# The last RMS norm of a decoder trunk: column-wise Newton steps, and one of four final products on GpSimd

## The chip, the cores and the metric

The kernel runs on one core of a Trainium2 chip. The metric is the device time of one execution, in microseconds (us); of several runs the median is given. The profile is of one execution, taken by the hardware profiler. Its engines are called PE (TensorE), DVE (VectorE), ACT (ScalarE), POOL (GpSimd) and SP (SyncE), and L143 means line 143 of the kernel.

## The reference

The reference computes one layer of a decoder trunk for 1024 tokens of width 1024 in float32: an attention part of three head groups, a gated MLP with a short convolution, a gated per-layer embedding, and a last RMS norm. Only the end matters here:

```python
gate = jax.nn.sigmoid(_rmsnorm(r, ple_norm[i]).astype(dt) @ w_ple_gate[i])
r = r + (p[i] @ w_ple_proj[i]) * gate
...
return _rmsnorm(r, final_norm).astype(dt)
```

where `_rmsnorm` multiplies each token's row by one over the root of its mean square (plus 1e-6), and by a gain per feature.

## The kernel before, in words

The activations are held feature-major: eight tiles of 128 features by 1024 tokens (`r[d]`, two of them in each tile `r2[i]`). Every float32 matrix product is made of three matmuls on split operands (`mm3`, L115 to L119).

The last stage works on three pieces of the tokens, 512, 256 and 256 wide (`PIECES`). `embed` (L1134) computes a piece: for each of the eight feature tiles d it makes the gate's matmuls on PE into a PSUM tile `pg` (L1163), and `gate_in` (L1140) scales the result, takes the sigmoid on ACT, multiplies by the embedding, adds it to `r[d]` (L1145), gathers the squares (L1147, the last tile's at L1149), and multiplies `r[d]` by the gain of the last norm on ACT (L1151).

`finish` (L1174) then ends a piece. It is called for a piece while the next piece's matmuls run (by `before()` behind the second feature tile, L1169), and for the last piece alone at the very end (L1188). It does the following:

- `rms_sum` (L146): matmuls with a column of ones bring the sum of squares of each token into a PSUM tile, 128 tokens on the partitions and one column per 128 tokens (L152, L154). So a piece of 256 tokens has two columns. L157 makes the mean.
- `rsqrt` (L132): one over the root on VectorE by a first guess from the bits (L135, L137), a halved and negated input `h` (L139), and three Newton iterations of three operations each (L141 to L143), each of which needs the one before it. The working tile is `t`, the result is `y`.
- `rms_spread` (L161): a matmul for each column against the identity puts the result, one factor per token, on all 128 partitions of a PSUM tile (L166).
- Four products on VectorE, each over two feature tiles (128 partitions x 2 x 256 elements), multiply `r2` by that PSUM tile in place (L1179), and after each SP issues the store of 256 KB (L1181).

`rsqrt` is also used with four and eight columns, earlier in the kernel and in the first piece. The framework lets every engine work through its own queue in order; it chooses the order of the queues by priorities, which follow the order in which the program states the operations, and puts a wait where two operations touch the same tile and one of them must come first.

Other lines that the prediction speaks of: L536 and L537 (part of the rotary embedding; ACT copies a PSUM tile into `t`, VectorE multiplies the same PSUM tile into `z`), L619 and L620 (ACT copies, and VectorE masks, a PSUM tile into the two halves of `pT`), L346 (the running states of the two recurrent heads, one with a decay per partition read from SBUF as the tile `fs`, the other with a constant), L605 (a two-column operation with a scalar per partition), L781 (a sum of squares, on GpSimd in earlier stages).

Of the kernel before, what the change touches and what calls it, by code (L numbers as in the profile page):

```python
# [22 lines left out]
ALU = mybir.AluOpType  # L23
# [3 lines left out]
P = 128  # L27
T = 1024
D = 1024
KD = D // P  # L30
# [5 lines left out]
PIECES = ((0, 512), (512, 768), (768, 1024))  # L36
# [39 lines left out]
def trunk(ctx: ExitStack, tc: tile.TileContext, a, out, dbg):  # L76
    nc = tc.nc
    V, S, G, TE = nc.vector, nc.scalar, nc.gpsimd, nc.tensor
# [4 lines left out]
    ps = ctx.enter_context(tc.tile_pool(name="ps", bufs=1, space=PSUM))  # L83
# [11 lines left out]
    def half(h):  # L95
        return slice(h * H2, (h + 1) * H2)
# [35 lines left out]
    def rsqrt(y, v, n, pool):  # L132
        h = pool.tile([P, n], F32, tag="rq_h", bufs=2, name="rq_h")
        t = pool.tile([P, n], F32, tag="rq_t", bufs=2, name="rq_t")
        V.tensor_scalar(out=t.bitcast(I32), in0=v.bitcast(I32), scalar1=1, scalar2=None,  # L135
                        op0=ALU.logical_shift_right)
        V.tensor_scalar(out=y.bitcast(I32), in0=t.bitcast(I32), scalar1=-1.0, scalar2=float(0x5F3759DF),  # L137
                        op0=ALU.mult, op1=ALU.add)
        V.tensor_scalar(out=h, in0=v, scalar1=-0.5, scalar2=None, op0=ALU.mult)  # L139
        for _ in range(3):  # L140
            V.tensor_tensor(out=t, in0=y, in1=y, op=ALU.mult)  # L141
            V.tensor_tensor(out=t, in0=t, in1=h, op=ALU.mult)
            V.scalar_tensor_tensor(out=y, in0=t, scalar=1.5, in1=y, op0=ALU.add, op1=ALU.mult)  # L143


    def rms_sum(acc, cols, name, rest=None):  # L146

        n = (cols.stop - cols.start) // P
        pt = b1(f"ss_{name}")
        for c in range(n):  # L150
            ac = slice(cols.start + c * P, cols.start + (c + 1) * P)
            TE.matmul(pt[:, c:c + 1], acc[:, ac], ones[:, 0:1], start=True, stop=rest is None)  # L152
            if rest is not None:
                TE.matmul(pt[:, c:c + 1], rest[:, ac], ones[:, 0:1], start=False, stop=True)  # L154
        v = cp.tile([P, 8], F32, tag="rb_v", bufs=2, name=f"rb_v{name}")
        y = cp.tile([P, 8], F32, tag="rb_y", bufs=2, name=f"rb_y{name}")
        V.tensor_scalar(out=v[:, :n], in0=pt[:, :n], scalar1=1.0 / D, scalar2=EPS, op0=ALU.mult, op1=ALU.add)  # L157
        rsqrt(y[:, :n], v[:, :n], n, cp)
        return y[:, :n]
# [9 lines left out]
    def rms_bc(acc, rs, cols, name, rest=None):  # L169

        y = rms_sum(acc, cols, name, rest)
        n = y.shape[-1]
        for c0 in range(0, n, 4):
            m = min(4, n - c0)
            pb = rms_spread(y[:, c0:c0 + m], name)
            if rs is None:
                return pb
            S.copy(rs[:, cols.start + c0 * P:cols.start + (c0 + m) * P], pb)
# [25 lines left out]
    with tc.high_priority(offset=100000):  # L204
# [4 lines left out]
        for k in range(KD):  # L209
            x = xs[k]  # L210
# [9 lines left out]
            for h in range(2):  # L220
                S.mul(hi[:, half(h)], x[:, half(h)], col(C_G1 + k))
                V.scalar_tensor_tensor(out=lo[:, half(h)], in0=x[:, half(h)], scalar=col(C_G1 + k),
                                       in1=hi[:, half(h)].bitcast(F32), op0=ALU.mult, op1=ALU.subtract)
# [8 lines left out]
            for n in range(NS):  # L232
                for h in range(2):
                    w = slice(n * P, n * P + P)
# [79 lines left out]
    def head_out(po, dst):  # L314

        pv = po.rearrange("p (c d) -> p c d", c=NC)
        sq = ap.tile([P, NC, 64], F32, tag="kt", bufs=1, name="hsq")
        S.square(sq, pv)
        v = ap.tile([P, NC], F32, tag="hv", bufs=2, name="hv")
        y = ap.tile([P, NC], F32, tag="hy", bufs=2, name="hy")  # L320
        V.tensor_reduce(out=v, in_=sq, axis=AX.X, op=ALU.add)
        V.tensor_scalar(out=v, in0=v, scalar1=1.0 / 64, scalar2=EPS, op0=ALU.mult, op1=ALU.add)
        rsqrt(y, v, NC, ap)
        V.tensor_tensor(out=dst.rearrange("p c (e d) -> p (c e) d", e=2), in0=pv,
                        in1=y[:, :, None].to_broadcast([P, NC, 64]), op=ALU.mult)
# [434 lines left out]
    def f4(tag, name, shape=(P, T), dt=F32):  # L760
        if tag == "big":
            return big.tile(list(shape), dt, tag="big", name=name)
        if tag in ("wraw", "whi", "wlo"):
            return wp.tile(list(shape), dt, tag=tag, bufs=1 if tag == "wraw" else 2, name=name)
        return fp.tile(list(shape), dt, tag=tag, bufs=BUFS[tag], name=name)
# [73 lines left out]
    for d in range(KD):  # L839
        out_tile_half(d, 1)  # L840
        if d == 0:
            y = rms_sum(acc2, half(0), "r0")
# [8 lines left out]
    for n, (h, i, d) in enumerate((h, i, d) for h in range(2) for i in range(2) for d in range(4)):  # L851
# [9 lines left out]
        if n == 1:  # L861
            with tc.high_priority(offset=100):
                y = rms_sum(acc2, half(1), "r1")
# [170 lines left out]
    def weights_down(src, n, name):  # L1034
        with tc.high_priority(offset=400):
            raw, hi, lo = [f4(t, f"wd{name}{t}", (P, n, P), dt)
                           for t, dt in (("wraw", F32), ("whi", F32R), ("wlo", F32R))]
            nc.sync.dma_start(raw, src)
            hl(hi, lo, raw)
        return hi, lo  # L1040
# [4 lines left out]
    def streamed(f, again):  # L1045
        return h3_parts(f, again, *[f4("r", f"{c}3{f}{again}", dt=F32R) for c in "hl"])

    def kept(f):
        if f == NF - 1 or f == NF - 2:
            t = f4("hx", f"h3{f}", (P, 2, T), F32R)  # L1050
            return h3_parts(f, 0, t[:, 0], t[:, 1])
        return h3_parts(f, 0, *[f4("big", f"{c}3{f}", dt=F32R) for c in "hl"])
# [5 lines left out]
    r2 = []  # L1058
# [39 lines left out]
    for f in range(NF):  # L1098
        x = streamed(f, 0) if f < NR else kept(f)
        h3[f] = x  # L1100
        w = weights_down(a["w_dn0"][f], 4, f"a{f}")
# [9 lines left out]
    for n, f in enumerate([*range(NR, NR + NE), *range(NR)]):  # L1111
        x = streamed(f, 1) if f < NR else h3[f]
        w = weights_down(a["w_dn1"][f], 4, f"b{f}")
# [7 lines left out]
    for d in range(4):  # L1121
        w = weights_down(a["w_dn2"][d], NK, f"c{d}")
# [51 lines left out]
    def finish(n, t0, t1):  # L1174
        c = slice(t0, t1)
        w = t1 - t0
        pb = rms_bc(acc4[0][:, c], None, slice(0, w), f"f{n}", last_sq[n])
        for d in range(0, KD, 2):
            V.tensor_tensor(out=r2[d // 2][:, :, c], in0=r2[d // 2][:, :, c],  # L1179
                            in1=pb[:, None, :].to_broadcast([P, 2, w]), op=ALU.mult)  # L1180
            nc.sync.dma_start(out[d:d + 2, :, c].rearrange("d p t -> p d t"), r2[d // 2][:, :, c])  # L1181

    last_sq = []
    before = None
    for n, (t0, t1) in enumerate(PIECES):
        embed(n, t0, t1, before)
        before = functools.partial(finish, n, t0, t1)
# [116 lines left out]
```

## Time and profile before

| what | value |
| --- | --- |
| median of three runs | 1291.88 us (lowest 1289.81, highest 1574.35) |
| profiled execution, its own time | 1289.75 us |
| span from first to last instruction | 1288.0 us |
| mean granted clock of PE | 0.995 |
| instructions | 16291 |

A row of the timeline gives the start and the length in us, the engine, the line, the operation, output and inputs with their shapes, and in brackets the time that the engine stood idle before it and what ended this. A row of one line's view gives the shortest, median and longest duration in ns, and under it what the engine waited for (us in total, times, or us, times, longest). A row of the stretches gives for each stretch its length, each engine's busy time, the clock granted to PE, the busy share of the 16 DMA engines and the GB/s they moved. A row of the DMA issues gives the number of transfers, the size of one and the time from issue to landing.

### The profile page before, as it was taken

The numbers are of one execution on the slowest core, as the hardware profiler recorded it, in microseconds if no ns is written. First come the engines' busy times: TensorE is split into PE (matmuls) and PEld (weight loads), VectorE is DVE, ScalarE is ACT, GpSimd is POOL, SyncE is SP. The second block draws the span as 40 slices with busy tenths as digits, with TensorE's granted clock in tenths as the row PEclk, the third lists the DMA queues.
The fourth block names the chain that finished last, engine by engine and source line by source line (L and its number), as shares of the span: only waits on it lengthen the run. The fifth ranks groups of instructions, "written<-read, shape, count | busy, mean of one in ns | idle before, by whom it ended". The sixth has DMA issues, their size and how long they took to land.

```text
span 1288.0 us, 16291 instructions
## 1 busy us (share of the span) xinstructions
PE 1262.1 (98%) x6330; PEld 1058.9 (82%) x6330; DVE 838.7 (65%) x1410; ACT 536.9 (42%) x842; POOL 103.8 (8%) x113
## 2 busy tenths in 40 slices
PE   9999999999999999999999999999999999999996
PEld 7888888888888887788788888888888888888896
DVE  7986967567676477967776776677456123346576
ACT  7324143257674256544444344334245123334432
POOL 2000000012111231000000000000000021001010
PEclk9999999999999999999999999999999999999998
DMA  7110110111013745222223122123457216323132
GB/s 249 50 34 17 34 33 19 49 33 34 17 34 122 284 135 180 82 98 77 87 82 98 66 82 98 68 88 100 162 163 255 72 53 201 106 90 115 41 107 83
DMA packets 42239, 122.31 MB, mean 95 GB/s; under 512 B 5169, under 2 KB 7729, under 8 KB 42161
## 3 DMA queue, kind: packets, MB, share of 16 engines
q1 hardware_dynamic: 32032, 89.14, 21.3%
q0 software_dynamic: 8544, 30.41, 6.4%
q10 hardware_dynamic: 1584, 1.71, 0.4%
q8 instruction: 50, 0.82, 0.3%
q14 instruction: 29, 0.23, 0.1%
HBM read 97.13 MB, written 24.12 MB: 94 GB/s over the span
## 4 chain that ended last, share of the span: by engine, by line
PE 69%; issue 11%; POOL 2%; DVE 1%; ACT 1%; DMA 0%; DVEq 0%; POOLq 0%; ACTq 0%
PE d L118 6%; PE d L117 6%; PE d L119 6%; PE gb L117 3%; PE gb L118 3%; PE gb L119 3%; PE pg L117 2%; PE gd L117 2%; PE gd L118 2%; PE pg L119 2%; PE gd L119 2%; PE pg L118 2%; PE ga L118 2%; PE ga L119 2%; PE ga L117 2%
## 5 line engine op out<-in xcount | busy, mean ns | idle before, releaser
L117 PE MATMUL ga<-b,whig 128*128 128x512 f32 x176 | 68.9, 392 | 0.3
L119 PE MATMUL ga<-b,wlog 128*128 128x512 f32 x176 | 68.6, 390 | 0.5 <-DVE wlog L773 0.5
L117 PE MATMUL gb<-b,f 128*128 128x512 f32 x176 | 68.7, 390 | 0.0
L118 PE MATMUL ga<-b,whig 128*128 128x512 f32 x176 | 68.6, 390 | 0.0
L119 PE MATMUL gb<-b,f 128*128 128x512 f32 x176 | 68.5, 389 | 0.0
L118 PE MATMUL gb<-b,f 128*128 128x512 f32 x176 | 68.5, 389 | 0.0
L117 PE MATMUL pg<-hp,hpg 128*128 128x256 f32 (+1 forms) x192 | 61.7, 321 | 0.0
L773 DVE TENSOR_TENSOR l<-h3r,h 128x1024 fp32r<-128x1024 f32 x32 | 38.8, 1224 | 34.5 <-ACT h L772 34.5
L119 PE MATMUL pg<-hp,lpg 128*128 128x256 f32 (+1 forms) x192 | 61.0, 318 | 0.0
L118 PE MATMUL pg<-lp,hpg 128*128 128x256 f32 (+1 forms) x192 | 61.0, 318 | 0.0
L772 ACT CAST h<-h3r 128x1024 fp32r<-128x1024 f32 x34 | 35.3, 1050 | 41.1 <-PE d L118 19.7
L955 ACT ACTIVATE cv<-cv 128x1024 f32<-128x1024 f32 x22 | 23.4, 1062 | 67.8 <-DVE cv L953 67.7
L946 DVE TENSOR_TENSOR us<-us,s 128x512 f32<-128x512 f32 x21 | 14.5, 691 | 50.9 <-ACT us L945 50.9
L987 POOL DMA_DIRECT2D h3d<-us x22 | 11.8, 535 | 417.6 <-DVE us L986 417.6
L781 POOL TENSOR_TENSOR acc<-acc,sq 128x512 f32<-128x512 f32 (+1 forms) x15 | 29.0, 1936 | 166.1 <-ACT sq L780 165.8
L117 PEld LDWEIGHTS ga<-b,whig 128*128 128x128 f32 x176 | 33.0, 188 | 8.9 <-ACT s L972 1.5
L945 ACT COPY us<-gd 128x512 f32<-128x512 f32 x22 | 12.9, 588 | 64.2 <-DMA h3d<-us 63.6
L119 PEld LDWEIGHTS ga<-b,wlog 128*128 128x128 f32 x176 | 33.0, 188 | 7.9 <-DVE wlog L773 1.0
L117 PEld LDWEIGHTS gb<-b,f 128*128 128x128 f32 x176 | 33.0, 188 | 7.4 <-DVE us L939 0.3
L119 PEld LDWEIGHTS gb<-b,f 128*128 128x128 f32 x176 | 33.0, 188 | 6.9
L118 PEld LDWEIGHTS pg<-lp,hpg 128*128 128x128 f32 x192 | 36.6, 191 | 2.6 <-DVE lp L1081 0.2
L119 PEld LDWEIGHTS pg<-hp,lpg 128*128 128x128 f32 x192 | 36.6, 190 | 2.5
(778 smaller groups left out, 3859.2 us busy)
## 6 DMA issues: line engine op xcount, KB each, us to landing
wu<-w_gu SPq DMA_DIRECT2D x22, 512.0 KB, 3.5
wg<-w_gu SPq DMA_DIRECT2D x22, 512.0 KB, 3.5
h3d<-us POOLq DMA_DIRECT2D x22, 512.0 KB, 2.9
h3r<-h3d SPq DMA_DIRECT2D x22, 512.0 KB, 3.7
wr_wo<-w_out SPq DMA_DIRECT2D x16, 512.0 KB, 3.7
h3r<-h3d POOLq DMA_DIRECT2D x12, 512.0 KB, 3.8
x<-xT SPq DMA_DIRECT2D x16, 256.0 KB, 5.4
r<-xT SPq DMA_DIRECT2D x16, 256.0 KB, 7.2
```

What stands on the lines that cost most here:

```text
L117: TE.matmul(o, wh, xh, start=first, stop=False, skip_group_check=on)
L118: TE.matmul(o, wh, xl, start=False, stop=False, skip_group_check=on)
L119: TE.matmul(o, wl, xh, start=False, stop=last, skip_group_check=on)
L772: S.copy(hi, src)
L773: e.tensor_tensor(out=lo, in0=src, in1=hi.bitcast(F32), op=ALU.subtract)
L781: e.tensor_tensor(out=acc[:, cols], in0=acc[:, cols], in1=sq[:, cols], op=ALU.add)
L945: S.copy(u1, bank["d"])
L946: V.tensor_tensor(out=u1, in0=u1, in1=s1, op=ALU.add)
L955: S.activation(cv, cv, AF.Gelu_apprx_tanh)
L987: G.dma_start(h3_dram[f], us)
```

## The change

Two edits, both at the end of a piece.

In `rsqrt`, when there are at most two columns (the second and the third piece of the last norm), the two operations y*y and (y*y)*h are replaced by one for each column, which takes that column of `h` as a scalar per partition: (y*h)*y. The third operation of an iteration stays as it is.

In `finish`, for the last piece only, ScalarE first copies the spread factors from PSUM into an SBUF tile `ps`. The product of feature tiles 6 and 7 is made by GpSimd with this copy, and its store is issued by ScalarE's queue. It is stated second, so the order in the program is 0, 6, 2, 4; the other three products stay on VectorE with the PSUM tile, and their stores on SP.

```diff
         for _ in range(3):
-            V.tensor_tensor(out=t, in0=y, in1=y, op=ALU.mult)
-            V.tensor_tensor(out=t, in0=t, in1=h, op=ALU.mult)
+            if n <= 2:
+                for c in [slice(i, i + 1) for i in range(n)]:
+                    V.scalar_tensor_tensor(out=t[:, c], in0=y[:, c], scalar=h[:, c], in1=y[:, c],
+                                           op0=ALU.mult, op1=ALU.mult)
+            else:
+                V.tensor_tensor(out=t, in0=y, in1=y, op=ALU.mult)
+                V.tensor_tensor(out=t, in0=t, in1=h, op=ALU.mult)
             V.scalar_tensor_tensor(out=y, in0=t, scalar=1.5, in1=y, op0=ALU.add, op1=ALU.mult)
...
         pb = rms_bc(acc4[0][:, c], None, slice(0, w), f"f{n}", last_sq[n])
-        for d in range(0, KD, 2):
-            V.tensor_tensor(out=r2[d // 2][:, :, c], in0=r2[d // 2][:, :, c],
-                            in1=pb[:, None, :].to_broadcast([P, 2, w]), op=ALU.mult)
-            nc.sync.dma_start(out[d:d + 2, :, c].rearrange("d p t -> p d t"), r2[d // 2][:, :, c])
+        if n == len(PIECES) - 1:
+            ps = f4("ws", "rs4")[:, :w]
+            S.copy(ps, pb)
+        for d in (0, 6, 2, 4) if n == len(PIECES) - 1 else range(0, KD, 2):
+            e, x = (G, ps) if d == 6 and n == len(PIECES) - 1 else (V, pb)
+            e.tensor_tensor(out=r2[d // 2][:, :, c], in0=r2[d // 2][:, :, c],
+                            in1=x[:, None, :].to_broadcast([P, 2, w]), op=ALU.mult)
+            (S if e is G else nc.sync).dma_start(out[d:d + 2, :, c].rearrange("d p t -> p d t"), r2[d // 2][:, :, c])
```

## The prediction

> **What bounds the kernel now.** I read the page's first part, then the timeline of the last 15 us, then the DMA engines by half microsecond, then single lines.
>
> ```profile
> span 1288.0 us, 16291 instructions
> PE 1262.1 (98%) x6330; PEld 1058.9 (82%) x6330; DVE 838.7 (65%) x1410; ACT 536.9 (42%) x842; POOL 103.8 (8%) x113
> ```
>
> TensorE is the bound, so an edit on another engine can only count where TensorE waits for it. That is the end, after the last gate product:
>
> ```profile
> 1277.37 0.57 PE L154 MATMUL ss_f<-ones,pt 128*128 128x1 f32 x2
> ...
> 1278.17 0.17 DVE L135 TENSOR_SCALAR rq_t<-rb_vf 128x2 int32<-128x2 int32 x1
> 1278.25 0.16 DVE L139 TENSOR_SCALAR rq_h<-rb_vf 128x2 f32<-128x2 f32 x1
> 1278.37 0.17 DVE L137 TENSOR_SCALAR rb_yf<-rq_t 128x2 int32<-128x2 int32 x1
> 1278.58 0.16 DVE L141 TENSOR_TENSOR rq_t<-rb_yf 128x2 f32<-128x2 f32 x1
> 1278.77 0.16 DVE L142 TENSOR_TENSOR rq_t<-rq_t,rq_h 128x2 f32<-128x2 f32 x1
> 1278.97 0.16 DVE L143 SCALAR_TENSOR_TENSOR rb_yf<-rq_t,rb_yf 128x2 f32<-128x2 f32 x1
> 1279.16 0.16 DVE L141 TENSOR_TENSOR rq_t<-rb_yf 128x2 f32<-128x2 f32 x1
> ...
> 1280.14 0.16 DVE L143 SCALAR_TENSOR_TENSOR rb_yf<-rq_t,rb_yf 128x2 f32<-128x2 f32 x1
> ...
> 1280.45 1.19 PE L166 MATMUL rb_f<-ident,rb_yf 128*128 128x128 f32 x4 [2.51 <-DVE rb_yf L143]
> 1281.68 2.48 DVE L1179 TENSOR_TENSOR rr<-rr,rb_f 128x512 f32<-128x512 f32 x4 [1.38 <-PE rb_f L166]
> 1282.43 2.13 SPq L1181 DMA_DIRECT2D out<-rr  x4
> ```
>
> Here everything is one chain. A step that depends on the one before starts 0.195 us after it (0.16 of work, 0.035 of handover); one that doesn't starts 0.08 after it (L135, L139). An iteration is three dependent steps, 1278.58 to 1279.16: 0.585 us, and three make 1.755. Then the spread on TensorE, four products 0.60 apart (2.48 less the last one's 0.69, over three), and a store behind each. What ends the chain is not the last product:
>
> ```profile
> 1283.50:1284.00 0.50, 0.00 (x0) 0.00 (x0) 0.50 (x2) 0.00 (x0) 0.00 (x0) 0.50 1.05 342
> ...
> 1285.50:1286.00 0.50, 0.00 (x0) 0.00 (x0) 0.00 (x0) 0.00 (x0) 0.00 (x0) 0.50 1.01 348
> 1286.00:1286.50 0.50, 0.00 (x0) 0.00 (x0) 0.00 (x0) 0.00 (x0) 0.00 (x0) 0.50 0.81 279
> ```
>
> The last two columns are the busy share of the 16 DMA engines and GB/s. From 1283.5, before the third product is done, to about 1286.4 the engines are full. The stores' queue and the last store:
>
> ```profile
> q1 hardware_dynamic: 1088, 1.05, 44.7%
> ```
>
> ```profile
> 1284.19 0.37 SPq L1181 DMA_DIRECT2D out<-rr  x1
> ```
>
> ```profile
> out<-rr SPq DMA_DIRECT2D x1, 256.0 KB, 2.7
> ```
>
> 1.05 MB at 345 GB/s take 3.0 us. The last store, issued at 1284.19, lands 2.7 later at 1286.9; 1.1 us of closing waits follow. So the end is set by when the first store is issued (1282.43), plus 4.47 us of a stream at full rate, not by the products behind it.
>
> **The change part by part.**
>
> *The copy to SBUF.* GpSimd takes its factor from a copy that ScalarE makes of the spread result, and in the program that copy stands ahead of all four products. Do the products on VectorE, which read the same PSUM tile, wait for it? In L537 VectorE reads a PSUM tile that ScalarE's L536 copies, and writes another tile than L536 does; in L619 and L620 ScalarE and VectorE read one tile too.
>
> ```profile
> L537 DVE TENSOR_TENSOR ck<-z_ck,cosT x4: 691/692/692, 123.3 to 204.1; 128x512 f32<-128x512 f32 x4
> ...
>   ACT tbq L536: 13.9, 7
> ```
>
> ```profile
> 300.34 0.37 ACT L619 COPY pT<-tb 128x256 f32<-128x256 f32 x1 [0.97 <-PE tb L617]
> ...
> 300.74 0.42 DVE L620 TENSOR_TENSOR pT<-tb,tmask 128x256 f32<-128x256 f32 x1 [0.87 <-ACT pT L619]
> ```
>
> L537's own data came from TensorE alone, and yet it waited seven times, 13.9 us, for ScalarE's reading of the tile. So two readers of a PSUM tile go one after the other, in the order of the program. L619 is just the copy that is added (128x256 from PSUM): VectorE starts 0.40 after it. Bounds: 0 if the products may start beside it, +0.60 if the handover costs half as much again as the copy. I take +0.40: first product at 1282.08, first store at 1282.83.
>
> The Trainium skill (PSUM — Partial Sum Buffer, PSUM bank collisions raise a hardware error) says that two engines may not touch one bank and the same partitions at once, reading against reading included. The trace agrees by L537's 13.9 us; with the rule the term is 0.40, without it 0, and it lowers the chance of the rival that lets them run side by side.
>
> *Newton with two columns.* L141 and L142 go, and two column steps come, each with a scalar per partition read from SBUF; the count of instructions stays nine. If these cost what plain ones do, an iteration is 0.08 + 0.195 + 0.195 = 0.47 and three save 0.35. But the scalar read from SBUF costs:
>
> ```profile
> L346 DVE SCALAR_TENSOR_TENSOR sta<-sta,fs,ua x24: 273/280/289, 111.2 to 184.8; 64x64 f32<-64x64 f32 x24
> L346 DVE SCALAR_TENSOR_TENSOR stc<-stc,uc x24: 202/220/226, 207.6 to 250.8; 64x64 f32<-64x64 f32 x24
> ```
>
> ```profile
> 292.72 0.35 DVE L605 TENSOR_SCALAR bmx<-sb,nsink 128x2 f32<-128x2 f32 x2
> ```
>
> ```profile
> 292.72 0.21 DVE L605 TENSOR_SCALAR bmx<-sb,nsink 128x2 f32<-128x2 f32 x1
> ```
>
> The same operation takes 0.06 us more with such a scalar (280 against 220 ns). L605 is a two-column operation with one: 0.21 long, and the second of a pair ends 0.35 after the first began, so it began some 0.13 after it. An iteration is then 0.35 to the end of the second column step, 0.035 of handover and 0.195 of the last step: 0.58, against 0.585. I take -0.02 for all three. Bounds: -0.35 without the extra, and +0.35 if the second column step has to wait for the first, since both write tile t (2 x 0.255 + 0.195 = 0.705 an iteration).
>
> *The same Newton in the piece before*, whose chain runs beside TensorE:
>
> ```profile
> 1259.52 0.15 DVE L143 SCALAR_TENSOR_TENSOR rb_yf<-rq_t,rb_yf 128x2 f32<-128x2 f32 x1
> 1259.57 0.28 PE L119 MATMUL pg<-hp,lpg 128*128 128x256 f32 x1
> ...
> 1259.81 0.68 PE L166 MATMUL rb_f<-ident,rb_yf 128*128 128x128 f32 x4
> ```
>
> Matmuls there start 0.12 apart, and the spread starts 0.24 after the one before, so TensorE stands 0.12 for the chain. An earlier result gains at most 0.12; one later by 0.35 costs 0.35. The nine steps lie between VectorE's gate work, which sets most of their starts: I take 0, from -0.12 to +0.35.
>
> *One product on GpSimd, its store by ScalarE's queue.*
>
> ```profile
> L781 POOL TENSOR_TENSOR acc<-acc,sq x15: 1290/1715/2732, 415.8 to 1159.2; 128x512 f32<-128x512 f32 x10, 128x1024 f32<-128x1024 f32 x5
> ```
>
> The product has L781's shape of 512 elements: 1.29 to 1.72 us there. It starts with the first VectorE product, after the copy: 1282.1 to 1283.8, its store at some 1283.9. That falls between the second and third store of SP (1282.83, 1283.43, 1284.03), so the DMA engines, filled from 1283.9 by 0.75 us of data with each store, are never empty, and the stream takes its 4.47 us from the first store as before. VectorE ends 0.60 earlier than with four products, and this buys nothing: it was the data that came last. What hides GpSimd is this stream: the three stores of SP keep it full until about 1286.1, and a store needs 1.1 us from issue to its first data, so GpSimd may end as late as 1284.9, a product of 2.8 us. SP's queue loses one issue of 0.37 that lay beside the stream. Behind ScalarE's wait for the product nothing is queued. 0, from -0.3 (two queues pack better) to +0.5.
>
> The Trainium skill (DMA: Bandwidth & Descriptors, Issuing engines are not separate DMA queues) holds that stores begun from several engines end up on the same 16 engines and save only issue time. By that rule the term is 0; read as a queue's own limit, the 0.7 us between landings would leave a gain of as much. The share of 1.05 in the row above is for the rule.
>
> *The sum.* 1289.75 us for the profiled execution, 1288.0 of it span: +0.40 (copy) - 0.02 (Newton) + 0 + 0 = 1290.13. The runs shown have 1291.88 as median and 1289.81 as lowest, so the profiled one lies at the low end, and a median falls up to 2 us above it. I put the median of the changed kernel 0.5 above the sum: 1290.6.
>
> **The rivals.**
>
> *Side by side.* The copy delays nobody and the columns cost no extra: the first store moves 0.35 forward and the time is 1290.6 - 0.38 - 0.35 = 1289.9. For it: the operands of the products come from TensorE alone. Against it: L537, and L346's 60 ns.
>
> *The columns go one by one* (slower). Both column steps write t and may be held apart. The price is 0.35 in the last piece, up to as much in the one before, on top of the copy: 1290.6 + 0.37 + 0.2 = 1291.2. It decides from the point where a column step starts more than 0.14 after the other. Against it: L605's pair overlaps.
>
> *GpSimd comes last* (slower). If its product takes over 2.8 us, its store is alone at the end. At 3.5 us it would cost 0.7: 1291.3. For it: L781 spreads from 1.29 to 1.72 by what runs beside it. Against it: 2.73 is its longest, and that at twice the size. The Trainium skill (SBUF — State Buffer, Who interferes with whom) has GpSimd held while VectorE reads two operands from SBUF; the three products here read one from SBUF and one from PSUM. No row here has such a pair.
>
> *It does not do what it says.* "Two dependent steps" hold for dependence, not for time; this is the forecast's own Newton term.
>
> **How the numbers follow.** Forecast 0.62; side by side, whole or half, 0.18; columns one by one 0.12; GpSimd last 0.08. The terms of all lie between -0.8 and +1.2 us around the sum; the median's place among runs adds up to 2 us upward and 0.3 downward. From the sum of 1290.13 that is 1289.0 to 1292.8. A measurement of this kernel can tell about 2% from no change, 26 us, and no case comes near: same 0.98, 0.01 each for what the cases don't hold.
>
> **What would show it.** Right: the copy at the end of the spread, the first product 0.40 after its start; column steps of 0.21 and an iteration near 0.58; the GpSimd product of 1.3 to 1.8 us, its store ahead of SP's last; DMA engines full from the first data on; 4.4 to 4.5 us from first issue to last landing. Wrong: VectorE's first product beside the copy, an iteration of 0.47 or 0.70, a gap in the stream, or a last landing that belongs to ScalarE's store alone.

## The result and the profile after

The changed kernel takes 1292.65 us as the median of 22 runs, the kernel before 1291.08 us as the median of 22. The ratio is 1.0013, with a 95% interval of 1.0007 to 1.0019: the change costs 0.9 to 2.5 us. That is far below 2%, but it is not nothing, and it is about four times the 0.4 us that the sum of the prediction gave. One of the 22 runs of the change, at 5166.26 us, lies far off the rest, and the ratio leaves it out.

The profiled execution took 1294.32 us. The first lines of its page:

```profile
span 1292.5 us, 16293 instructions
PE 1264.3 (98%) x6330; PEld 1061.0 (82%) x6330; DVE 838.3 (65%) x1409; ACT 537.3 (42%) x843; POOL 104.9 (8%) x114
```

One instruction moved from DVE to POOL, and one copy came on ACT, as the diff says. The end in the timeline of the changed kernel (start and length in us; from L143 on the lines lie five later than before, in `finish` nine):

```profile
1280.55 0.16 DVE L162 TENSOR_SCALAR rb_vf<-ss_f 128x2 f32<-128x2 f32 x1 [0.92 <-PE ss_f L159]
...
1281.15 0.35 DVE L143 SCALAR_TENSOR_TENSOR rq_t<-rb_yf,rq_h 128x1 f32<-128x1 f32 x2
1281.54 0.16 DVE L148 SCALAR_TENSOR_TENSOR rb_yf<-rq_t,rb_yf 128x2 f32<-128x2 f32 x1
1281.73 0.35 DVE L143 SCALAR_TENSOR_TENSOR rq_t<-rb_yf,rq_h 128x1 f32<-128x1 f32 x2
...
1283.00 1.20 PE L171 MATMUL rb_f<-ident,rb_yf 128*128 128x128 f32 x4 [2.49 <-DVE rb_yf L148]
1284.24 0.37 ACT L1185 COPY rs<-rb_f 128x256 f32<-128x256 f32 x1 [4.06 <-PE rb_f L171]
1284.64 1.88 DVE L1188 TENSOR_TENSOR rr<-rr,rb_f 128x512 f32<-128x512 f32 x3 [1.78 <-ACT rs L1185]
1284.70 1.26 POOL L1188 TENSOR_TENSOR rr<-rr,rs 128x512 f32<-128x512 f32 x1 [15.90 <-ACT rs L1185]
1285.36 1.60 SPq L1190 DMA_DIRECT2D out<-rr  x3
1285.99 0.48 ACTq L1190 DMA_DIRECT2D out<-rr  x1
```

This is nearly the end that was forecast: the copy, VectorE 0.40 us behind the copy's start and released by it, an iteration of 0.58 us, a GpSimd product of 1.26 us, and ScalarE's store ahead of SP's last: it is issued at 1285.99 together with SP's second, where the forecast had it between the second and the third. The DMA engines in the last 6 us of the changed kernel, in stretches of half a microsecond and one of 2.5 (the last two columns are their busy share and GB/s):

```profile
1286.50:1287.00 0.50, 0.00 (x0) 0.00 (x0) 0.02 (x1) 0.00 (x0) 0.00 (x0) 0.50 1.02 313
...
1289.00:1289.50 0.50, 0.00 (x0) 0.00 (x0) 0.00 (x0) 0.00 (x0) 0.00 (x0) 0.50 0.72 248
1289.50:1290.00 0.50, 0.00 (x0) 0.00 (x0) 0.00 (x0) 0.00 (x0) 0.00 (x0) 0.50 0.00 0
1290.00:1292.50 2.50, 0.00 (x0) 0.00 (x0) 0.00 (x0) 0.00 (x0) 0.00 (x0) 0.50 0.00 0
```

The last data have landed by about 1289.8, 4.47 us after the first issue at 1285.36. Then, for 2.7 us, no engine computes and no data move. Before, 1.1 us lay between the last landing and the end. What fills the additional 1.6 us is in the rows of the closing line, the last line of the program, which the pages count as no work. A DRAIN there is an instruction with which an engine closes: VectorE's of the kernel before lasts 2514 ns from 1281.7, as long as its four products (2.48 us). The closing line of the changed kernel (shortest, median and longest duration in ns, first and last start in us):

```profile
L1308 POOLq EVENT_SEMAPHORE  x4: 17/17/17, 1291.8 to 1292.4; - x4
L1308 POOLq DRAIN  x3: 40/93/7120, 1284.7 to 1292.3; - x3
L1308 SPq DRAIN  x3: 7/7/7, 1290.1 to 1292.0; - x3
```

The same of the kernel before:

```profile
L1299 POOLq EVENT_SEMAPHORE  x4: 17/17/17, 1287.2 to 1287.9; - x4
L1299 POOLq DRAIN  x3: 40/102/6550, 1264.9 to 1287.7; - x3
L1299 SPq DRAIN  x3: 7/7/7, 1287.1 to 1287.5; - x3
L1299 DVEq DRAIN  x2: 19/1266/2514, 1281.7 to 1287.5; - x2
```

SP has walked through its waits and drains at 1290.1; GpSimd, which leads the exchange of semaphores that ends the kernel, joins only at 1291.8, when its own first DRAIN of 7.12 us, begun at 1284.65, is over. That DRAIN begins when GpSimd's last instruction begins, and reaches 5.8 us past that instruction's end (7.12 less 0.05 and the product's 1.26). Before, GpSimd's last instruction was a DMA issue 23 us ahead of the end, in the timeline of the kernel before:

```profile
1264.90 0.72 POOL L1158 DMA_DIRECT2D ppt<-ppd  x1 [6.79 <-DVE pt L1144]
```

Its DRAIN was over at 1271.4, under TensorE's gate matmuls, and SP came last. So GpSimd's DRAIN goes on for 5.8 us behind its last instruction, and the change moved that last instruction from 1264.9 to 1284.7.

To compare kernels without what lies ahead of the end, I count the tail: from the start of the last mean step on VectorE (L157, L162 in the change: `rb_vf<-ss_f`) to the end of the span. The tail was 10.00 us (1277.98 to 1287.97) and is 11.99 us (1280.55 to 1292.54). In it the copy has 0.40, Newton has -0.02, and the DRAIN the rest: the exchange begins 1.72 us after SP's first closing DRAIN (9.54 and 11.26 us after the mean step) where it began 0.09 after it (9.17 and 9.26), which is 1.63 more.

The two profiled executions differ by 4.57 us, so 2.6 us more lie ahead of the tail. There TensorE's granted clock fell to half for 3.4 us, twice, at 69 and 536 us, far ahead of anything that the change touches. Stretches of the changed kernel (after the busy times of the five engines stands the granted clock):

```profile
69.00:71.00 2.00, 2.00 (x8) 1.73 (x8) 2.00 (x4) 0.97 (x1) 0.00 (x0) 0.50 0.00 0
71.00:73.00 2.00, 2.00 (x7) 1.59 (x6) 1.94 (x5) 1.15 (x2) 0.00 (x0) 0.66 0.00 0
...
536.00:538.00 2.00, 2.00 (x7) 1.53 (x6) 1.55 (x2) 0.00 (x0) 0.00 (x0) 0.64 0.55 219
538.00:540.00 2.00, 2.00 (x6) 1.61 (x5) 1.70 (x3) 1.04 (x1) 0.00 (x0) 0.50 0.00 0
```

The kernel before had 1.00 in both places. Half of twice 3.4 us is 3.4 us of matmul time; against it, the last sums ran at full clock in the changed kernel (3.17 us from the last gate product on VectorE at 1277.38 to the mean step, where it was 3.78 from 1274.20), which gives back 0.6. Of the kernels below that leave the code there alone, the profiles show no such stretch (`pool_last`), one (`newton_only`, `pool_at_y`) or two (`no_gpsimd`, `copy_second`, `eight_stores`, `warm`, `warm_seven`), with and without GpSimd in the end. So I take them for what varies between executions; that is argued, not shown. The trace of before speaks for it too: just ahead of the first place TensorE was as idle as in the changed kernel, and its clock stayed full. The rows, the changed kernel's first and then that of before:

```profile
66.00:69.00 3.00, 1.07 (x10) 0.90 (x9) 3.00 (x7) 1.98 (x2) 0.00 (x0) 0.99 0.00 0
66.00:69.00 3.00, 1.06 (x9) 0.90 (x9) 3.00 (x6) 1.73 (x2) 0.00 (x0) 1.00 0.00 0
```

The Trainium skill (TensorE: Matmul & The Clock Gate, What's actually happening) says that the clock is halved after an idle window of about 3.4 us, that it is full again after a busy one, and that the windows run on whatever the kernel does. The length of the stretches, 3.4 us, agrees with the busy window; the idle time just ahead of the first was shorter, 1.93 us (66.46 to 68.39).

### The profile page after: what moved, and what is told of

Same layout as the page of the kernel before. It is cut to its first block, busy times and chain, and to the rows that moved or that the text cites. A ratio compares the mean times of both kernels' runs of the same rounds, so it can differ in the third digit from the quotient of the medians.

```text
span 1292.5 us, 16293 instructions
## 1 busy us (share of the span) xinstructions
PE 1264.3 (98%) x6330; PEld 1061.0 (82%) x6330; DVE 838.3 (65%) x1409; ACT 537.3 (42%) x843; POOL 104.9 (8%) x114
## 4 chain that ended last, share of the span: by engine, by line
PE 68%; issue 11%; POOL 2%; DVE 1%; ACT 1%; DMA 0%; DVEq 0%; POOLq 0%; ACTq 0%
PE d L118 6%; PE d L117 6%; PE d L119 6%; PE gb L118 3%; PE gb L117 3%; PE gb L119 3%; PE pg L117 2%; PE gd L117 2%; PE gd L118 2%; PE pg L119 2%; PE pg L118 2%; PE gd L119 2%; PE ga L118 2%; PE ga L119 2%; PE ga L117 2%
## 5 line engine op out<-in xcount | busy, mean ns | idle before, releaser
L117 PEld LDWEIGHTS gb<-b,f 128*128 128x128 f32 x176 | 33.5, 190 | 7.3 <-DVE gs L944 0.2
L118 PEld LDWEIGHTS gb<-b,f 128*128 128x128 f32 x176 | 33.5, 190 | 7.0
L119 PEld LDWEIGHTS gb<-b,f 128*128 128x128 f32 x176 | 33.3, 189 | 7.0
```

The costliest lines, as they stand in the source:

```text
L117: TE.matmul(o, wh, xh, start=first, stop=False, skip_group_check=on)
L118: TE.matmul(o, wh, xl, start=False, stop=False, skip_group_check=on)
L119: TE.matmul(o, wl, xh, start=False, stop=last, skip_group_check=on)
```

## The experiments

The main theory after the result: GpSimd's closing DRAIN sets the end, because GpSimd's last instruction is now late. Rivals: the product and its store, or the copy, cost more than their rows show; or the end is late because the stores go through two queues. This table has the tail of every kernel, in us after the start of the last mean step, as read from the traces. "SP done" is the start of SP's first closing DRAIN, "GpSimd done" the end of GpSimd's first one, "exchange" the start of GpSimd's closing semaphores.

| kernel | first product | first store issued | SP done | GpSimd done | exchange | end |
| --- | --- | --- | --- | --- | --- | --- |
| before | 3.70 | 4.45 | 9.17 | -6.56 | 9.26 | 10.00 |
| the change | 4.09 | 4.80 | 9.54 | 11.22 | 11.26 | 11.99 |
| no_gpsimd | 4.09 | 4.80 | 9.52 | -5.96 | 9.61 | 10.34 |
| newton_only | 3.68 | 4.43 | 9.16 | -5.96 | 9.25 | 9.97 |
| copy_second | 3.68 | 4.43 | 9.60 | 11.94 | 11.98 | 12.71 |
| pool_last | 3.71 | 4.46 | 9.16 | 14.95 | 14.99 | 15.71 |
| pool_at_y | 3.70 | 4.46 | 9.16 | 8.39 | 9.25 | 9.99 |
| no_pool_dma | 3.70 | 4.46 | 9.99 | 10.03 | 10.08 | 10.74 |
| few_pool_dma | 3.71 | 4.47 | 9.31 | 9.92 | 9.97 | 10.70 |
| change_no_pool_dma | 4.09 | 4.81 | 9.53 | 5.47 | 9.62 | 10.29 |
| eight_stores | 3.70 | 4.15 | 9.12 | -6.21 | 9.21 | 9.94 |
| warm | 3.19 | 3.64 | 8.61 | -5.97 | 8.70 | 9.43 |
| warm_seven | 3.19 | 3.64 | 8.16 | -5.97 | 8.25 | 8.98 |

Each row is of one profiled execution. In every row the exchange begins 0.04 to 0.05 us after GpSimd is done or 0.09 after SP is done, whichever is later.

**The change without GpSimd** (`no_gpsimd`). Product 6 on VectorE with the same copy, its store still on ScalarE's queue.

```diff
-            e, x = (G, ps) if d == 6 and n == len(PIECES) - 1 else (V, pb)
+            e, x = (V, ps) if d == 6 and n == len(PIECES) - 1 else (V, pb)
...
-            (S if e is G else nc.sync).dma_start(out[d:d + 2, :, c].rearrange("d p t -> p d t"), r2[d // 2][:, :, c])
+            (S if x is not pb else nc.sync).dma_start(out[d:d + 2, :, c].rearrange("d p t -> p d t"), r2[d // 2][:, :, c])
```

> The change with its GpSimd product given back to VectorE: copy, order, Newton columns and the store on ScalarE's queue stay; product 6 reads the copy in SBUF. Measured from the start of the mean step (L157 of before) to the end of the span, before has 10.0 us and the change 12.0. Theory (GpSimd's closing drain lasts 5.8 us from its last instruction and outlasts the stores by 1.6 us): GpSimd's last instruction is early again, 10.4 us, which is the copy's 0.40 alone; ratio to before 1.0003. Rival (it is the store on ScalarE's queue, or its closing, that costs): 12.0 us as in the change, ratio 1.0013.

Measured: a tail of 10.34 us, the median 1290.40, and a ratio to before of 0.9993 (0.9983 to 1.0003). GpSimd's closing rows of this kernel:

```profile
L1308 POOLq EVENT_SEMAPHORE  x4: 17/17/17, 1289.1 to 1289.7; - x4
L1308 POOLq DRAIN  x3: 40/102/6548, 1267.0 to 1289.6; - x3
```

The DRAIN is long, but early again, and 1.65 us of the tail are gone. The copy and the second queue are still there: they make the 0.34 over before, which the ratio's interval only just holds. The first rival falls for the store and the copy, the last rival falls too.

**Newton alone** (`newton_only`): before, with the diff's edit in `rsqrt` and nothing else.

> Before with the two-column Newton steps alone. Theory (a scalar read from SBUF costs 0.06 us and pushes the second column step to 0.137 after the first): an iteration of 0.58 as before, 10.0 us from the mean step to the end, ratio 1.000. Rival (fewer dependent steps shorten the chain): 9.65 us. Rival (a cost in the piece before, where the chain runs beside TensorE): up to 0.35 us of standing TensorE there, ratio 1.0003.

Measured: first product 3.675 us after the mean step where it was 3.702, a tail of 9.97, a median of 1290.13 and a ratio of 0.9991 (0.9982 to 1.0000). The column steps are worth 0.03 us in the last piece.

**The copy behind the first product** (`copy_second`). The copy's 0.40 us can be taken off the first store by stating it later; GpSimd then starts later.

```diff
-        if n == len(PIECES) - 1:
-            ps = f4("ws", "rs4")[:, :w]
-            S.copy(ps, pb)
         for d in (0, 6, 2, 4) if n == len(PIECES) - 1 else range(0, KD, 2):
+            if d == 6 and n == len(PIECES) - 1:
+                ps = f4("ws", "rs4")[:, :w]
+                S.copy(ps, pb)
```

> The change with the copy to SBUF stated behind the first VectorE product and not ahead of all four. The first store is issued 0.40 us earlier, GpSimd's product starts 0.69 us later. Theory (GpSimd's drain sets the end): 12.0 + 0.7 = 12.7 us from the mean step to the end. Rival (the copy's delay of the first store sets the end): 11.6 to 12.0 us.

Measured: a tail of 12.71 us, a median of 1294.00 and a ratio of 1.0018 (1.0007 to 1.0028). Timeline and closing line of `copy_second`:

```profile
1283.22 0.69 DVE L1188 TENSOR_TENSOR rr<-rr,rb_f 128x512 f32<-128x512 f32 x1 [1.38 <-PE rb_f L171]
1283.94 0.37 ACT L1186 COPY rs<-rb_f 128x256 f32<-128x256 f32 x1 [4.78 <-DVE rr L1188]
1283.97 2.10 SPq L1190 DMA_DIRECT2D out<-rr  x3
1284.35 1.28 DVE L1188 TENSOR_TENSOR rr<-rr,rb_f 128x512 f32<-128x512 f32 x2 [0.44 <-ACT rs L1186]
1284.40 1.26 POOL L1188 TENSOR_TENSOR rr<-rr,rs 128x512 f32<-128x512 f32 x1 [16.62 <-ACT rs L1186]
```

```profile
L1308 POOLq DRAIN  x3: 40/93/7123, 1284.4 to 1292.0; - x3
```

It separates two answers well. The first store is issued 0.37 us sooner than in the change, and yet the end is 0.72 later, exactly as much as GpSimd's product starts later (4.86 against 4.15 after the mean step). In the change the end belongs to GpSimd and not to the stream of stores. The rows also show the readers of one PSUM tile going in the order of the program: the copy waits for the first product, and the second product for the copy.

**A small last instruction on GpSimd** (`pool_last`): before, with one GpSimd memset of one column at the very end. It writes zeros into a tile that has been stored by then, and nothing reads them.

```diff
     before()
+    G.memset(r2[3][:, 0, T - 1:T], 0.0)
```

> Before with one more instruction: GpSimd writes a zero to one element of each partition of the last stored tile, so it waits for that store to land; the output is not touched. Nothing else is added. Theory (the drain of 5.8 us follows any last GpSimd instruction): from the mean step 8.9 to the landing, 0.1 for the write, 5.8 of drain and 0.7 of closing: 15.6 us against 10.0; ratio 1.0043. Rival (the long drain belongs to a large product; a small write drains in 0.2 us as the writes at the kernel's start do): 10.2 us, ratio 1.0002.

Measured: the memset takes 0.10 us and starts at 1287.0, and the tail is 15.71: 5.7 us longer than before. The median is 1296.91, the ratio 1.0039 (1.0029 to 1.0050). Its closing line:

```profile
L1300 POOLq DRAIN  x3: 40/93/5930, 1287.0 to 1293.4; - x3
```

A tenth of a microsecond of work costs 5.7 us in the tail, and the interval of the ratio, 3.7 to 6.5 us, holds it. The DRAIN again reaches 5.8 us past the instruction's end.

**The same where there is room** (`pool_at_y`): before, with a GpSimd copy of the two columns of `y` into a tile that nobody reads, as soon as they are there.

```diff
         rsqrt(y[:, :n], v[:, :n], n, cp)
+        if name == f"f{len(PIECES) - 1}":
+            G.tensor_copy(cp.tile([P, 8], F32, tag="rb_z", bufs=1, name="rb_z")[:, :n], y[:, :n])
```

> Before with one small GpSimd instruction, a copy of the two-column Newton result into a scratch tile that nobody reads. It starts some 2.4 us after the mean step (L157). Theory (GpSimd's drain takes some 5.85 us behind its last instruction, whatever it was, and costs only what sticks out past the stores): drain over at 2.4 + 0.1 + 5.85 = 8.4, before SP is done at 9.2, so 10.0 us from the mean step to the end as before. Rival (a GpSimd instruction this late costs in itself, by its drain or by its reading beside VectorE): over 10.3 us.

Measured: the copy (0.18 us) starts 2.40 us after the mean step, its DRAIN of 6.02 us is over at 8.39, SP is done at 9.16, and the tail is 9.99. One run: 1290.33 us. A late GpSimd instruction is free as long as it ends 5.8 us ahead of SP's closing; here 0.8 us of room were left.

**Where the 5.8 us come from** (`no_pool_dma`, `few_pool_dma`). The kernel issues 70 DMAs from GpSimd. `no_pool_dma` is `pool_last` with all of them on SP, in five lines such as

```diff
-            G.dma_start(h3_dram[f], us)
+            nc.sync.dma_start(h3_dram[f], us)
```

and `few_pool_dma` puts the eight stores of L860 back on GpSimd.

> The kernel pool_last (one small GpSimd write behind the last landing) with every DMA of the GpSimd queue issued by SP, so that GpSimd issues no DMA in the whole kernel; the middle may become slower, the end is what is looked at. Theory A (the long drain clears up behind GpSimd's own DMA queue): it shrinks to some 0.2 us as at the kernel's start, and mean step to end is 10.0 us. Theory B (the closing drain of GpSimd is long whatever it did): 5.8 us of drain and 15.7 us to the end, as in pool_last.

> The kernel no_pool_dma (one small GpSimd write behind the last landing) with the eight stores of the embedding's product (L860, early in the gated MLP) back on GpSimd's queue, 8 DMAs in place of 70. Theory A1 (any use of the queue makes the closing drain long): 5.8 us. Theory A2 (the drain grows with the DMAs issued, 5.8 us for 70): some 0.8 us.

Measured, the closing rows of `pool_last`'s GpSimd in the two, `no_pool_dma` first:

```profile
L1300 POOLq DRAIN  x3: 34/78/181, 1289.2 to 1289.8; - x3
```

```profile
L1300 POOLq DRAIN  x3: 40/102/867, 1288.7 to 1290.1; - x3
```

GpSimd's queue in the view of DMA queues (packets, MB, us x engines share) of `few_pool_dma`, and the same of `pool_last`:

```profile
q0 software_dynamic: 1152, 4.19, 0.9%
```

```profile
q0 software_dynamic: 8544, 30.41, 6.3%
```

Past the memset's 0.10 us the DRAIN lasts 0.07 us with no DMA from GpSimd, 0.75 with 8 and 5.8 with 70: 0.08 us for each DMA that GpSimd has issued in the kernel, however long ago (the last of the 8 was issued at 511 us). Less the 0.07, it fits the count of DMAs (0.686 / 8 = 0.086, 5.75 / 70 = 0.082 us) better than the packets (0.60 and 0.67 ns each). These are three counts, one trace each, and what the DRAIN does in this time is not shown. In `no_pool_dma` the tail missed its number: it is 10.74, since one of SP's four final issues took 1.37 us in place of 0.37 (3.02 us for the four in place of 2.13; why stays open), the memset waited for the later landing, and SP was done at 9.99. The DRAIN itself stays short, as the first theory had it. The times (one run each, 1291.88 and 1292.33) say nothing of the end, since SP issues other transfers too.

**The whole change, without DMAs from GpSimd** (`change_no_pool_dma`): the diff's kernel, with the same five lines on SP.

> The change whole, with every DMA of the GpSimd queue issued by SP instead; the middle may become slower, the end is what is looked at. Theory (the long drain clears up behind GpSimd's own DMA queue, and in the change it is what ends last): the drain behind the GpSimd product is 0.2 us, and mean step to end is 12.0 - 1.6 = 10.4 us with the GpSimd product still in place. Rival (a drain behind a large GpSimd product is long anyway): 12.0 us.

Measured: a tail of 10.29 us with the GpSimd product in its place (1.27 us at 1284.64), the closing row of this kernel:

```profile
L1308 POOLq DRAIN  x3: 34/78/1371, 1284.6 to 1290.5; - x3
```

The DRAIN is the product and 0.10 us, and 1.70 us of the tail are gone. So it isn't the product that is late but what GpSimd's queue leaves to its end. As a whole this version is no gain: its one run took 1293.17 us.

**The stream itself, in smaller stores** (`eight_stores`). By the prediction the first issue sets the end. Before, with the last piece in eight products of 128x256 and eight stores, by SP and ScalarE in turn:

```diff
+        else:
+            for d in range(KD):
+                V.tensor_tensor(out=r[d][:, c], in0=r[d][:, c], in1=pb, op=ALU.mult)
+                (S if d % 2 else nc.sync).dma_start(out[d, :, c], r[d][:, c])
```

> Before with the last piece's four products as eight of half the size, each stored at once, the stores taken in turn by SP's and ScalarE's queue; no GpSimd, no copy, Newton as before. Theory (the end is the first store's issue plus a stream of 4.47 us at full rate): the first store is issued 0.27 us sooner (a product of 0.42 in place of 0.69), products come 0.335 apart and bring 0.37 us of stream each, so 9.7 us from the mean step to the end against 10.0. Rival (more and smaller stores stretch the stream or the closing): 10.0 or more.

Measured: the first issue is 0.30 us sooner (4.15 against 4.45), and SP sees the last store landed at 8.62, which is 4.47 after the first issue, as predicted; yet the tail is 9.94 and not 9.7. That is a miss. The single records of SP's closing waits in the traces show why: they ask for one or two semaphores each, in a fixed order, 0.06 us apart. In `eight_stores` the last store to land stands in the second of them, and seven more follow (8.68 to 9.05); before, it stood in the sixth, and three followed (8.99 to 9.11). So SP is done 0.49 us after it sees the last landing, where it was 0.25, and most of the 0.30 is spent there. The median is 1291.40, the ratio 1.0007 (0.9998 to 1.0016).

**TensorE kept busy through the end** (`warm`, `warm_seven`). The spread took 1.19 us at half clock in the last piece and 0.68 in the piece before it. `warm` is `eight_stores` with matmuls that nobody reads ahead of the sums and ahead of the spread:

```diff
+            warm(c, 16)
+            y = rms_sum(acc4[0][:, c], slice(0, w), f"f{n}", last_sq[n])
+            pw = b1("warm2")
+            for _ in range(10):
+                TE.matmul(pw[:, :P], ident, last_sq[n][:, :P], start=True, stop=True)
+            pb = rms_spread(y, f"f{n}")
```

`warm_seven` has one whole store in place of the last two halves, so that the last semaphore stands last in SP's order.

```diff
-            for d in range(KD):
+            for d in range(KD - 2):
...
+            V.tensor_tensor(out=r2[3][:, :, c], in0=r2[3][:, :, c],
+                            in1=pb[:, None, :].to_broadcast([P, 2, w]), op=ALU.mult)
+            nc.sync.dma_start(out[KD - 2:KD, :, c].rearrange("d p t -> p d t"), r2[3][:, :, c])
```

> eight_stores with matmuls into a tile that nobody reads in the two gaps of TensorE at the end, so that it isn't idle before the sums and the spread. Theory (in before the clock is granted at half from 1276.2 on, two us after TensorE fell idle, and the spread takes 1.21 us where it would take 0.64): 9.15 us from the mean step to the end, and up to 0.4 us less ahead of it; ratio 0.9990. Rival (the granted clock falls in spite of the filling, or the filling delays the sums): 9.7 us or more.

> warm with seven stores in place of eight: the last two halves are one product and one store again. SP's closing waits go through the stores' semaphores in a fixed order, 0.06 us each; in eight_stores and warm the last store's stands second, so seven more are walked after its landing, with seven stores it stands last. Theory: 0.4 us less than warm, 9.0 us from the mean step to the end against 10.0 in before, and 0.5 less ahead of it; ratio 0.9990. Rival (the last landing itself is later with the larger last store): 9.4 us as in warm.

Measured: tails of 9.43 and 8.98 us. The timeline of `warm_seven`:

```profile
1282.42 0.68 PE L166 MATMUL rb_f<-ident,rb_yf 128*128 128x128 f32 x4 [0.17 <-DVE rb_yf L143]
1283.14 2.08 DVE L1198 TENSOR_TENSOR rr<-rr,rb_f 128x256 f32<-128x256 f32 x6 [0.87 <-PE rb_f L166]
1283.59 1.66 SPq L1199 DMA_DIRECT2D out<-rr  x3
1283.92 1.66 ACTq L1199 DMA_DIRECT2D out<-rr  x3
...
1285.84 0.38 SPq L1202 DMA_DIRECT2D out<-rr  x1
```

The granted clock in the spread, 1.00 in `warm` (first row) and 0.50 in `eight_stores`:

```profile
1281.60:1282.40 0.80, 0.68 (x4) 0.52 (x4) 0.00 (x0) 0.00 (x0) 0.00 (x0) 1.00 0.00 0
1282.90:1284.20 1.30, 1.19 (x4) 0.93 (x4) 0.02 (x1) 0.00 (x0) 0.00 (x0) 0.50 0.00 0
```

The spread takes 0.68 us, the first store is issued 3.64 us after the mean step where it was 4.15 in `eight_stores` and 4.45 in before, and in `warm_seven` SP is done 0.45 sooner than in `warm` with the same first issue: the order of the waits accounts for most of the miss of `eight_stores` and of `warm`. `warm` misses its 9.15 by 0.28, most of it for that reason; its median is 1289.75, its ratio 0.9996 (0.9987 to 1.0005). The median of `warm_seven` is 1289.99 (11 runs), the ratio to before 0.9994 (0.9985 to 1.0003): the gain of 1.0 us in the tail is there in the trace, and the runs can't tell it from nothing. Its interval lies below that of the change.

## Why the prediction was right and wrong, point by point

- **The copy, +0.40: right.** The first product starts 4.088 us after the mean step, where it was 3.702. VectorE waits for ScalarE's reading of the same PSUM tile (1284.24, 1284.64), and `copy_second` shows the same in the other order. The rival "side by side" is out, and the Trainium skill's rule on two readers of a bank, named in the prediction, agrees with these rows.
- **Newton, -0.02: right.** Column steps of 0.220 and 0.213 us, the second 0.137 after the first, an iteration of 0.58 (1281.15 to 1281.73). Two dependent steps in place of three buy nothing, because a scalar per partition costs 0.06 us a step and the second column 0.14. "The columns go one by one" is out, though narrowly by its own mark: it was to decide above 0.14, and 0.137 is close to the 0.13 read from L605's pair.
- **The piece before, 0: right.** The spread there starts 0.24 us after the matmul ahead of it, as before (1262.99 after 1262.75).
- **The stream, 4.47 us from first issue to last landing: right.** It was 4.47 with two queues, and 4.47 with eight stores.
- **GpSimd, 0: wrong, and this is the step that failed.** The prediction said: "What hides GpSimd is this stream", and "GpSimd may end as late as 1284.9, a product of 2.8 us". The product took 1.26 us and its store came in time, as forecast. But the term followed the product to its store and stopped there. GpSimd's closing DRAIN goes on for 5.8 us after its last instruction. In the trace of the changed kernel SP is done at 1290.1, so the product would have had to end by 1284.3, before it had even begun (1284.70). This cost 1.63 us, outside the term's own -0.3 to +0.5. `no_gpsimd`, `pool_last`, `pool_at_y` and `change_no_pool_dma` show it from four sides.
- **"1.1 us of closing waits": wrong as a constant.** They are as long as the last engine needs. The row that says so, GpSimd's DRAIN of 6550 ns from 1264.9, stood in the trace of before, off the path, and I read only what was on it.
- **"GpSimd comes last": right in its name only.** It was to decide above a product of 2.8 us; the product was less than half of that. The range of 1.29 to 1.72 us behind it was misread: 1.72 is the median of two shapes, and the ten sums of 128x512 in the trace of before take 1.29 to 2.55.
- **The level, 1290.6.** Three errors beside the step above. The profiled execution of before (1289.75) lies 1.3 us below the median of its 22 runs, and I added only 0.5 for that. From 1291.08 the prediction's own terms give 1291.08 + 0.38 = 1291.5, and with the DRAIN's 1.63 it is 1293.1, against 1292.65 measured; the rest of 0.4 is within the interval of 0.9 to 2.5 us for the difference. And the number that I named, 1290.6, lay below the median shown, 1291.88, though the terms summed to a loss. The upper end of the range is a wrong sum as well: 1290.13 with +1.2 and +2 is 1293.3, not 1292.8.

## What to carry to other kernels

When work goes to an engine that had been done long before the end, look up how long that engine's closing wait lasts in the trace, and count its end from there, not from its last result. On GpSimd here this was 5.8 us, 0.08 us for each DMA that it had issued in the whole kernel; either its last instruction lies that far ahead of the end, or its DMAs are issued elsewhere. And set a sum that moves a median by tenths against the median of the runs, not against one profiled execution.

## What the runs showed of the hardware that was not expected

- GpSimd's first closing DRAIN grows with the DMAs it issued during the kernel: 0.07, 0.75 and 5.8 us past its last instruction with 0, 8 and 70 of them, even where the last of these was issued 20 us earlier.
- SP asks its closing semaphores in a fixed order, 0.06 us each, so that a store that lands last but stands early in the order costs up to 0.43 us after the landing.
- Matmuls that nobody reads, run through two gaps of 2.0 and 2.5 us, kept the granted clock at 1.00 where it was 0.50, and shortened the spread from 1.19 to 0.68 us.
